# Layer 2's attention and its products: the planner's order replaced by a pipeline laid by hand

## The chip, the cores and the metric

The kernel runs on one core of a Trainium2 chip. The metric is the device time of one execution in microseconds (us), as a median of several runs.

## What is computed

A two-layer encoder takes one step over T = 576 tokens: 512 new frames of one stream (the prompt) and 64 frames of another that has a past (the sample); the width is 2048. Layer 1 has stick-breaking attention beside a state-space branch. Layer 2 is what the change touches:

```python
def odd_layer(x, past_k, past_v, w_in, rel_bias, w_out, ln_g, ln_b):
    proj = jnp.einsum('bld,de->ble', x, w_in)
    q, k, v, g = jnp.split(proj, 4, axis=-1)
    ...
    o = chunk_band_attention(q, k, v, past_k, past_v, rel_bias).reshape(b_, L, CA_WIDTH) * jax.nn.silu(g)
    mix = jnp.einsum('ble,ed->bld', o, w_out)
    y = layer_norm(DEEPNORM_ALPHA * x + mix, ln_g, ln_b)
```

The attention has 32 heads of 64. Each frame sees its own chunk of 64 frames and the eight before; to the logits a bias by distance is added, then softmax, then the sum over the values. Outputs are y and the new caches of both layers.

## The kernel before

All products run on TensorE (PE) in single precision by halves: a weight `w` is split into `wh` (a copy rounded on ACT, L93) and `wl` (the rest, on DVE, L94), the input x into `yh` and `yl` likewise, and a product is the three terms wh·yh, wh·yl, wl·yh. Activations lie with features on partitions and tokens along the row, so a product of 128 features has 16 blocks of 128 inputs x 3 terms x two halves of 288 tokens: 96 matmuls.

Layer 2's attention runs over 16 pairs of heads. Queries and keys of all pairs have been made before and lie in memory; of the values only pairs 2, 5 and 8 (`VAHEAD`). So there are 29 products in this stage: 13 of values (v) and 16 of gates (g). `run_pairs` (L626) calls for each pair `ca_heads` (L1056: loads queries, keys and the sample's cache, makes the product v, copies it to `vf`, half on DVE at L1079 and half on ACT at L1080, stores it, and turns it to `vt` by transposes at L531 and L534), then `ca_gate` (L1150), then `ca_attend` (L1085). The gates of pairs 9, 11, 13 and 15 (`GLATE`) come after all pairs; the product with the attention's output is then done at the end.

`ca_attend` goes through seven parts: both heads' first 128 queries with the sample's new keys; the sample against its cache; both heads' second 128; and the third and fourth 128 of each head alone. For each part PE makes the logits `z` (L498, L499; the sample's at L504 and L1141), `softmax` takes the minimum of bias minus logits on DVE (L1115), the exponential with its sum on ACT (L1119), reciprocal (L1121) and scaling (L1123) on DVE; PE transposes the weights block by block (`tpw` at L594, the sample's at L600 and L606), and `evict` (L572) copies each transposed tile to `wts` or `wss`, in turn on DVE (L575) and ACT (L577). When all parts are done PE multiplies weights with values (`po` L614, `pos` L623), and `place` (L642) multiplies by the gate `gt` into `of` (L649, L656; without a gate a copy, L647 and L654), which is stored to `o_scr`.

The PSUM has eight banks of 512 columns. Four of them (`pj`) are three banks for halves of products (`product_halves`, L1015: first tokens 0 to 287 over all inputs, then the others) and one more for transposing (`spare`, in turn with the bank "t" by `tbank`, L580); the pool `pmc` has two for logits ("s"), one for transposing and the sample's `pos` ("t"), and one for `po` and the values' transposes ("o"). A gate is the silu of its product in six steps over ACT and DVE (`silu_halves`, L1032, the last at L1042).

The order on each engine is not that of the code: a planner takes, among the instructions that are ready by its own estimate of times, in order of the code's priority, so that products slide between the attention's instructions. What is written sets priorities, buffers and dependences. Behind the stage stands `mix_norm` (L750): it loads the stored outputs again (`bring`: `ol` at L773, split on ACT at L774 and DVE at L775), multiplies by `w_out` and normalises. The loads `ol8` to `ol15` go where the input x lay, which is free once the last product of the stage has been made.

Of the kernel before, what the change touches and what calls it, by code (L numbers as in the profile page):

```python
# [7 lines left out]
F32 = mybir.dt.float32  # L8
F32R = mybir.dt.float32r
AF = mybir.ActivationFunctionType  # L10
ALU = mybir.AluOpType
# [3 lines left out]
P = 128  # L15
# [34 lines left out]
def encoder(ctx: ExitStack, tc: tile.TileContext, a):  # L50
# [125 lines left out]
    def seven(wa, m0, wb, m1, sums, ps, tmp, last=False, early=None):  # L176
# [16 lines left out]

        a11, a21, a22 = raw(wa, m0, 0, "sr", tmp, 4), raw(wb, m1, 0, "sr", tmp, 4), raw(wb, m1, 1, "sr", tmp, 4)
        s_ = raw(None, 0, 0, "raw", wpool, 2)
        pa, pc = bank("pa", 2), bank("pc")
        o0, o1 = (tmp.tile([P, T], F32, tag="so", name="so", bufs=4) for _ in range(2))
# [374 lines left out]
    def evict(dst, src):  # L572
        flip[0] ^= 1
        if flip[0] & 1:
            nc.vector.tensor_copy(dst, src)  # L575
        else:
            act(dst, src, AF.Copy)  # L577

    spare = []

    def tbank(name):

        if spare:
            flip[0] ^= 2
            if flip[0] & 2:
                return spare[0]
        return pm.tile([P, 512], F32, tag="t", name=name)

    def transpose_tile(wsrc, r, t, wts, flipq=False):

        nb = t + 1
        tp = tbank("tpw")
# [5 lines left out]
    def transpose_new(wsrc, dst):  # L598
        tp = tbank("tpn")
# [3 lines left out]
    def transpose_cached(wsrc, dst):  # L603
        tp = tbank("tpw")
# [409 lines left out]
    turn_ = [0]  # L1014

    def product_halves(w, m):

        ws = [wparts(w, m, u) for u in range(2)]
        accs = []
        for v in (H0, H1):  # L1020
            acc = hbanks[turn_[0] % 3]
            turn_[0] += 1
            for u, (wh, wl) in enumerate(ws):
                for k in range(8):
                    c = slice(k * P, (k + 1) * P)
                    x, y = xh[8 * u + k][:, v], xl[8 * u + k][:, v]
                    for i, (st, mv) in enumerate(((wh, x), (wh, y), (wl, x))):
                        mm(acc, st[:, c], mv, start=(u == 0 and k == 0 and i == 0), stop=(u == 1 and k == 7 and i == 2))  # L1028
            accs.append((v, acc))
        return accs  # L1030

    def silu_halves(pl, accs, dst, tag):  # L1032
        t = pl.tile([P, 580], F32, tag=tag, name=tag, bufs=2)[:, :T]
        for v, p in accs:
            act(t[:, v], p, AF.Abs)
        act(t, t, AF.Exp, scale=-1.0)
        act(t, t, AF.Ln, bias=one1)
        for v, p in accs:
# [232 lines left out]
```

## Time and profile before

| what | us |
|---|---|
| median of 3 runs | 2790.82 (2788.62 to 2793.09) |
| the profiled execution | 2791.59 |
| its span, first to last instruction | 2789.8 |
| PE busy in the span | 2662.2 |
| layer 1's attention (695 to 1150): length, PE busy | 455.0, 449.16 |
| layer 2's attention with its products (1924.2 to 2547.5): length, PE busy | 623.3, 575.01 |
| from its last attention to `mix_norm`'s products (2487.6 to 2547.5): length, PE busy | 59.9, 48.98 |

Engines are PE (matmul), PEld (PE's loading of weights, beside it), DVE, ACT, POOL and SP. Matmuls are pipelined, so their durations overlap: the distance from one start to the next is what one costs. PEclk is TensorE's granted clock as a share of 2.4 GHz; its lower level is 1.2 GHz. "Idle before <- X" is the time that an engine stood still before an instruction, and X what ended it.

### The profile page before, as it was taken

The page shows a single profiled execution, that of the slowest core. Times are in us where ns is not written, and L with a number is a line of the kernel's source. Part 1 is how long each engine was busy: PE and PEld are TensorE (multiplying, and loading weights), DVE is VectorE, ACT ScalarE, POOL GpSimd, SP SyncE. Part 2 cuts the span into 40 slices and gives each one's busy share as a digit, 9 for nine tenths or more (in the row PEclk, how much of TensorE's full clock was granted, in tenths as well). Part 3 has the DMA queues.
Part 4 walks back from the last instruction along what each step waited for, and adds up shares of the span by engine and source line. Part 5 has one row for each costly group of instructions (what it writes and reads, how often), then busy time and mean ns, then how long its engine had stood idle before and what let it go on. Part 6 is the DMA issues. An engine that isn't in the chain of part 4 may idle for free.

```text
span 2789.8 us, 47678 instructions
## 1 busy us (share of the span) xinstructions
PE 2662.2 (95%) x19742; PEld 2538.9 (91%) x19742; DVE 1610.5 (58%) x2520; ACT 1190.2 (43%) x1993; POOL 63.4 (2%) x140
## 2 busy tenths in 40 slices
PE   8999999999999999999997799999999999989996
PEld 8999898999999999999997799999788888878995
DVE  6666656665666766733358377765554455443447
ACT  5434343443555655621136234444444444433224
POOL 0000000000000000000000000000000000000004
PEclk9999999999999999999998899999999999999998
DMA  5222222323323222533345465455644555434333
GB/s 184 76 90 76 71 94 65 101 70 117 97 90 99 93 90 92 191 106 101 94 129 186 138 210 161 158 162 179 199 152 147 155 159 162 143 107 139 104 102 134
DMA packets 148761, 350.36 MB, mean 126 GB/s; under 512 B 26304, under 2 KB 43968, under 8 KB 148544
## 3 DMA queue, kind: packets, MB, share of 16 engines
q1 hardware_dynamic: 105696, 281.68, 32.9%
q10 hardware_dynamic: 42848, 65.63, 6.3%
q8 instruction: 155, 2.54, 0.4%
q14 instruction: 62, 0.51, 0.1%
HBM read 281.63 MB, written 65.61 MB: 124 GB/s over the span
## 4 chain that ended last, share of the span: by engine, by line
PE 87%; DVE 5%; DMA 3%; ACT 3%; issue 2%; SPq 0%; ACTq 0%; DVEq 0%
PE pj L124 48%; PE pj L1028 13%; PE pa L159 5%; PE pc L159 3%; PE po L614 2%; PE pj L853 2%; PE pb L159 1%; PE tpw L594 1%; PE px L124 1%; ACT wh L93 1%; DVE wl L94 1%; PE z L498 1%; PE pos L623 1%; PE z L499 1%; DMA sr<-w_in 1%
## 5 line engine op out<-in xcount | busy, mean ns | idle before, releaser
L94 DVE TENSOR_TENSOR wl<-raw,wh 128x1024 fp32r<-128x1024 f32 x372 | 456.4, 1227 | 518.0 <-ACT wh L93 516.7
L93 ACT ACTIVATE wh<-raw 128x1024 fp32r<-128x1024 f32 x372 | 393.6, 1058 | 801.5 <-PE pj L124 498.1
L1028 PE MATMUL pj<-yh,wh 128*128 128x288 f32 x928 | 286.4, 309 | 18.9 <-DVE gt L1042 16.3
L1028 PE MATMUL pj<-yh,wl 128*128 128x288 f32 x928 | 283.7, 306 | 0.0
L1028 PE MATMUL pj<-yl,wh 128*128 128x288 f32 x928 | 282.9, 305 | 0.0
L1028 PEld LDWEIGHTS pj<-yh,wh 128*128 128x128 f32 x928 | 182.6, 197 | 27.5 <-DVE gt L1042 18.2
L124 PE MATMUL pj<-oh,wh 128*128 128x288 f32 x960 | 205.8, 296 | 0.0
L124 PE MATMUL pj<-ol,wh 128*128 128x288 f32 x960 | 205.8, 296 | 0.0
L124 PE MATMUL pj<-oh,wl 128*128 128x288 f32 x960 | 205.5, 295 | 0.0
L1028 PEld LDWEIGHTS pj<-yl,wh 128*128 128x128 f32 x928 | 182.3, 196 | 0.8
L1028 PEld LDWEIGHTS pj<-yh,wl 128*128 128x128 f32 x928 | 182.0, 196 | 0.5
L124 PEld LDWEIGHTS pj<-oh,wl 128*128 128x128 f32 x960 | 155.0, 188 | 0.0
L124 PEld LDWEIGHTS pj<-oh,wh 128*128 128x128 f32 x960 | 154.8, 188 | 0.2
L124 PEld LDWEIGHTS pj<-ol,wh 128*128 128x128 f32 x960 | 154.6, 188 | 0.0
L1119 ACT ACTIVATE t<-t,smx 128x128 f32<-128x128 f32 (+3 forms) x128 | 71.2, 557 | 88.4 <-DVE smx L1115 70.8
L1115 DVE CUSTOM_DVE_ANT_0 t<-z,bp 128x128 f32<-128x128 f32 (+3 forms) x128 | 60.2, 486 | 30.4 <-PE tpw L594 11.8
L498 PE MATMUL z<-kh,q 128*128 128x128 f32 (+1 forms) x192 | 66.5, 357 | 11.5 <-DVE smx L1115 9.3
L802 DVE TENSOR_TENSOR d<-xr,pj 128x576 f32<-128x576 f32 (+3 forms) x30 | 20.2, 673 | 91.5 <-PE pj L124 83.8
L93 ACT ACTIVATE wh<-sr 128x1024 fp32r<-128x1024 f32 x43 | 45.1, 1057 | 63.9 <-PE pc L159 23.2
L614 PE MATMUL po<-wts,vt 128*64 128x384 f32 (+3 forms) x384 | 70.8, 441 | 1.1 <-DVE wts L575 1.1
L577 ACT ACTIVATE wts<-tpw 128x128 f32<-128x128 f32 (+1 forms) x96 | 41.3, 430 | 60.9 <-PE tpw L594 53.5
L499 PE MATMUL z<-kl,q 128*128 128x128 f32 (+1 forms) x192 | 61.1, 328 | 0.0
(568 smaller groups left out, 7227.7 us busy)
## 6 DMA issues: line engine op xcount, KB each, us to landing
raw<-w_in SPq DMA_DIRECT2D x234, 512.0 KB, 3.6
raw<-w_out SPq DMA_DIRECT2D x95, 512.0 KB, 3.5
sr<-w_in SPq DMA_DIRECT2D x48, 512.0 KB, 4.3
ol<-o_scr SPq DMA_DIRECT2D x40, 288.0 KB, 5.4
xr<-xT SPq DMA_DIRECT2D x29, 288.0 KB, 5.8
q<-q_scr SPq DMA_DIRECT2D x64, 128.0 KB, 3.1
kh<-k_scr SPq DMA_DIRECT2D x64, 128.0 KB, 3.2
o_scr<-of ACTq DMA_DIRECT2D x24, 288.0 KB, 2.8
```

The lines of the kernel that those rows point to most:

```text
L93: act(hi, src, AF.Copy)
L94: tt(lo, src, hi.bitcast(F32), ALU.subtract)
L124: mm(ps[:, at.start + v.start:at.start + v.stop], st[:, c], mv[u * 8 + k][:, v], start=(first and k == 0 and i == 0), stop=(last and k == ...
L159: mm(acc, st[:, c], mv, start=(first and k == 0 and i == 0), stop=(k == 7 and i == 2), skip_group_check=more)
L498: mm(dst, q, kh, start=True, stop=False)
L499: mm(dst, q, kl, start=False, stop=True)
L577: act(dst, src, AF.Copy)
L614: mm(po[q, b * P:TP], vt[:, b, q], wts[:, b, r, b * P:TP], start=(b == 0), stop=(b == 3))
L853: mm(ps[i], st[:, c], mv, start=(u == order[0] and k == 0 and j == 0), stop=(u == 0 and k == 7 and j == 2))
L1028: mm(acc, st[:, c], mv, start=(u == 0 and k == 0 and i == 0), stop=(u == 1 and k == 7 and i == 2))
L1115: nc.vector.tensor_tensor_reduce(t[:, i, at:at + z.shape[1]], z, b, -1.0, 3e38 if j == 0 else sm[:, i:i + 1], ALU.add, ALU.min, sm[:, i:i ...
L1119: act(t[:, i, :], t[:, i, :], AF.Exp, scale=-1.0, bias=sm[:, i:i + 1], accum_out=sm[:, 2 + i:3 + i])
```

## The change

`ca_heads` only loads. All products come from a generator `ca_fill`, in the order v0 g0 v1 g1 g2 v3 g3 and so on, the four late gates at the end; it is advanced by an eighth of a product (12 matmuls) at a time. A product is made whole, both halves of 288 tokens in one tile of two banks, and two such tiles take the four banks of `pj`: the third half bank and the second transposing bank are gone. `ca_attend` calls `slot` after the logits and softmax of each part: it advances the generator by 13/7 of an eighth on the mean, and does the transposes that the slot before has left; the transposes of this part wait for the next slot. Values times weights and `place` of a pair (`finish`) are done in the first slot of the next pair. Gates have two buffers (`gt`) instead of one, the values' copy is one on DVE, silu goes over whole rows. Each late gate is multiplied in as soon as its product is there.

```diff
-        tp = tbank("tpw")
+        tp = pm.tile([P, 512], F32, tag="t", name="tpw")
...
-    x0, x1 = (pj.tile([P, 1024], F32, tag="pj", name="pj") for _ in range(2))
-    hbanks, second = [x0[:, 0:HALF], x0[:, 512:512 + HALF], x1[:, 0:HALF]], x1[:, 512:1024]
...
+    def ca_fill():
+        todo = []
+        for pr in range(NPAIR_CA):
+            todo += ([] if pr in VAHEAD else [("v", pr)]) + ([] if pr in GLATE else [("g", pr)])
+        for kind, pr in todo + [("g", pr) for pr in GLATE]:
+            ps = pj.tile([P, 1024], F32, tag="pj", name="pj")
+            toks, at = parts(HALF)
+            for u in range(2):
+                wh, wl = wparts(a["w_in1"], (32 if kind == "v" else 48) + pr, u)
+                for k in range(8):
+                    c = slice(k * P, (k + 1) * P)
+                    for i, (st, mv) in enumerate(((wh, xh), (wh, xl), (wl, xh))):
+                        for v in toks:
+                            mm(ps[:, at.start + v.start:at.start + v.stop], st[:, c], mv[u * 8 + k][:, v],
+                               start=(u == 0 and k == 0 and i == 0), stop=(u == 1 and k == 7 and i == 2))
+                    if k % 2 and (u, k) != (1, 7):
+                        yield
+            if kind == "v":
+                vf = ce_.tile([P, T], F32, tag="kvf", name="vf", bufs=2)
+                nc.vector.tensor_copy(vf, ps[:, at])
+                store(a["o_cav"][pr], vf)
+                yield
+                vts[pr] = turned_values(c_, vf)
+            else:
+                gt = cl_.tile([P, T], F32, tag="gt", name="gt", bufs=2)
+                silu(cl_, ps[:, at], gt, T, "st")
+                if pr in GLATE:
+                    tt(outs[pr], outs[pr], gt, ALU.mult)
+                    store(o_scr1[pr], outs[pr])
...
-            for i in range(np_):
-                transpose_tile(tv[:, i, :], seg[i][0], seg[i][1], wts, True)
+            slot([lambda i=i, tv=tv, seg=seg: transpose_tile(tv[:, i, :], seg[i][0], seg[i][1], weights()[0], True)
+                  for i in range(np_)])
...
+    def slot(work):
+        todo, later[:] = list(later), work
+        due[0] += 13
+        n, due[0] = due[0] // 7, due[0] % 7
+        for i in range(max(n, len(todo))):
+            if i < n:
+                next(fill, None)
+            if i < len(todo):
+                todo[i]()
...
+        finish = ca_attend(pr, st, slot)
+        later.append(finish)
+    slot([])
+    for _ in fill:
+        pass
```

On PE, the place in before that the trace shows at 2173.8 us: the transpose of a sample's new weights (L600), two heads' logits (L498, L499), transposes (L594), the next pair's first logits, and then a product again.

```order
L1028 MATMUL pj<-yh,wl 128x288
L600 MATMUL tpn<-cst,tsm 64x128
L498 MATMUL z<-kh_19286,q_21611 128x384
L499 MATMUL z<-kl_19288,q_21611 128x384
L498 MATMUL z<-kh_19287,q_21618 128x384
L499 MATMUL z<-kl_19289,q_21618 128x384
L594 MATMUL tpw<-cst,t 128x128 x6
L498 MATMUL z<-kh_19292,q_22032 128x128
L499 MATMUL z<-kl_19294,q_22032 128x128
...
L1141 MATMUL z<-kf,qb 128x64
L1028 MATMUL pj<-yh,wh 128x288
```

Such places stand between products that go by halves; the number of products' matmuls between two parts is the planner's.

On PE after the change, in the middle of the stage: two parts (L1131 ends the first's logits, L590 and L584 are transposes) with products (L1044) ahead of each transpose.

```order
L596 MATMUL tpw<-cst,tsm 128x128 x4
L498 MATMUL z<-kh_19290,q_22041 128x128
L499 MATMUL z<-kl_19292,q_22041 128x128
L498 MATMUL z<-kh_19291,q_22048 128x128
L499 MATMUL z<-kl_19293,q_22048 128x128
L1131 MATMUL z<-kf,qb 128x64
L1044 MATMUL pj<-yh,wl 128x288
...
L590 MATMUL tpn<-cst,tsm 64x128
L1044 MATMUL pj<-yl,wh 128x288 x2
...
L584 MATMUL tpw<-cst,t 128x128 x2
```

Some twenty matmuls of a product stand now between logits and the transposes that follow. Just ahead of that place, one of six stretches of the changed order in which the attention stands without products, where values times weights (L604, L613) of the pair before come too.

```order
L584 MATMUL tpw<-cst,t 128x128 x6
L604 MATMUL po<-wts,vt 64x512
L498 MATMUL z<-kh_19284,q_21653 128x384
L499 MATMUL z<-kl_19286,q_21653 128x384
L498 MATMUL z<-kh_19285,q_21660 128x384
L499 MATMUL z<-kl_19287,q_21660 128x384
L604 MATMUL po<-wts,vt 64x512
L604 MATMUL po<-wts,vt 64x384 x2
...
L613 MATMUL pos<-wss,cv 64x64 x8
L613 MATMUL pos<-wss,vt 64x64 x2
L531 MATMUL tpv<-cst,vf 128x128 x4
```

The products that stood here have moved ahead, and the stretch is 31 to 65 instructions long at its six places.

On DVE, before, at a gate's last step (L1042, two halves), between a part's softmax steps (L1115, L1123):

```order
L1123 TENSOR_SCALAR t<-t,smx 128x512
L1039 SCALAR_TENSOR_TENSOR st<-pj,st 128x288 x2
L1115 ISA t,smx<-z,bp_19301 128x384
L1115 ISA smx 128x1
L1042 TENSOR_TENSOR gt<-pj,st 128x288 x2
L575 COPY wts<-pj 128x128
```

and after, at the same step of a gate (L135, whole):

```order
L1113 TENSOR_SCALAR t<-t,smx 128x512
L1111 RECIPROCAL smx<-smx 128x1
L639 TENSOR_TENSOR of<-po,gt 128x512
L1113 TENSOR_SCALAR t<-t,smx 128x512
L646 TENSOR_TENSOR of<-pos,gt 128x64
L135 TENSOR_TENSOR gt<-pj,st 128x576
L575 COPY wts<-tpw 128x128
```

The gate's last step, which frees its product's banks, now stands behind `of` of an earlier pair, whose gate's buffer it takes.

On PE at the end of the stage, before: the last transposes and values of the attention, and then the late gates' products (286 matmuls from L1028 on).

```order
L594 MATMUL pj<-cst,t 128x128 x3
L623 MATMUL pos<-wss,cv 64x64 x8
L623 MATMUL pos<-wss,vt 64x64 x2
L614 MATMUL po<-wts,vt 64x512 x2
L614 MATMUL po<-wts,vt 64x384 x2
L614 MATMUL po<-wts,vt 64x256 x2
L614 MATMUL po<-wts,vt 64x128 x2
L1028 MATMUL pj<-yh,wh 128x288
```

and after: the last product's end (L1044), with what follows of pairs 13 to 15, and the first products of `mix_norm` (L124).

```order
L1044 MATMUL pj<-yh,wl 128x288 x2
L584 MATMUL tpw<-cst,t 128x128 x3
L604 MATMUL po<-wts,vt 64x512
L498 MATMUL z<-kh_19284,q_24722 128x384
...
L1131 MATMUL z<-kf,qb 128x64
...
L124 MATMUL pj<-oh_25775,wh 128x288 x4
...
L584 MATMUL tpw<-cst,t 128x128 x18
L604 MATMUL po<-wts,vt 64x512 x2
...
L124 MATMUL px<-oh_25775,wh 128x288 x2
```

The late gates' products have moved ahead of the last two pairs' attention, of which some 95 rows stand behind the last product.

## Rows read from the trace of the kernel before

**Rows 1.** The page: busy time of PE, and its clock in 40 slices.
```profile
PE 2662.2 (95%) x19742; PEld 2538.9 (91%) x19742; DVE 1610.5 (58%) x2520; ACT 1190.2 (43%) x1993; POOL 63.4 (2%) x140
...
PEclk9999999999999999999998899999999999999998
```

**Rows 2.** Windows: length, busy PE, PEld, DVE, ACT, POOL (x instructions), PEclk, DMA, GB/s.
```profile
695.00:1150.00 455.00, 449.16 (x3443) 427.48 (x3441) 301.35 (x469) 271.62 (x477) 0.00 (x0) 1.00 0.29 92
...
1924.20:2547.50 623.30, 575.01 (x4178) 520.88 (x4177) 307.88 (x862) 256.15 (x611) 2.00 (x6) 0.96 0.50 152
...
2487.60:2547.50 59.90, 48.98 (x338) 48.51 (x336) 21.16 (x30) 19.22 (x28) 0.00 (x0) 0.89 0.29 98
```

**Rows 3.** Windows: products alone, and the stage's products (L1028 only).
```profile
1890.00:1910.00 20.00, 20.00 (x153) 20.00 (x152) 14.67 (x19) 10.94 (x19) 0.52 (x1) 1.00 0.37 125
...
1924.20:2547.50 623.30, 414.75 (x2784) 392.46 (x2784) 0.96 0.50 152
```

**Rows 4.** PE's waits, us, times, longest: 1910 to 2550, then 695 to 1150.
```profile
PE pj L1028 <- DVE gt L1042: 16.3, 8, 6.0
PE z L498 <- DVE smx L1115: 9.3, 16, 1.5
PE tpw L594 <- ACT wss L577: 5.2, 7, 1.0
PE tpw L594 <- ACT wts L577: 4.9, 8, 1.5
PE pj L594 <- DVE wts L575: 3.0, 3, 1.5
...
PE pj L124 <- DVE kf L561: 3.4, 3, 1.1
```

**Rows 5.** Timeline of PE from 2173 us: start, duration, instruction, idle before it.
```profile
2173.76 0.27 PE L600 MATMUL tpn<-cst,tsm 128*64 128x128 f32 x1
...
2175.44 0.44 PE L594 MATMUL tpw<-cst,t 128*128 128x128 f32 x2 [0.71 <-ACT wss L577]
...
2179.66 0.40 PE L1028 MATMUL pj<-yh,wh 128*128 128x288 f32 x1 [1.12 <-DVE gt L1042]
2179.90 0.41 PE L1028 MATMUL pj<-yl,wh 128*128 128x288 f32 x1
```

**Rows 6.** Groups of DVE and ACT, 1924.2 to 2488: busy us, mean ns.
```profile
L1115 DVE CUSTOM_DVE_ANT_0 t<-z,bp 128x128 f32<-128x128 f32 (+3 forms) x128 | 60.2, 486 | 30.4 <-PE tpw L594 11.8 <-DMA bp<-relb 7.6 <-PE z L499 5.5
L1123 DVE TENSOR_SCALAR t<-t,smx 128x128 f32<-128x128 f32 (+3 forms) x128 | 46.1, 384 | 2.1
L575 DVE COPY wts<-pj 128x128 f32<-128x128 f32 (+1 forms) x64 | 31.1, 486 | 43.3 <-PE pj L594 43.1
...
L775 DVE TENSOR_TENSOR ol<-ol,oh 128x576 fp32r<-128x576 f32 x1 | 0.8, 757 | 0.0
...
L1119 ACT ACTIVATE t<-t,smx 128x128 f32<-128x128 f32 (+3 forms) x128 | 71.2, 557 | 88.4 <-DVE smx L1115 70.8 <-DMA ckr<-cak 9.8 <-DVE smx L1121 4.0
```

**Rows 7.** A window of 20 us, one of ten with a dip.
```profile
2370.00:2390.00 20.00, 17.47 (x108) 16.44 (x107) 6.58 (x15) 8.18 (x19) 0.00 (x0) 0.83 0.52 155
```

**Rows 8.** Windows: two stretches without products, and the last attention.
```profile
2066.00:2079.20 13.20, 9.92 (x62) 7.13 (x61) 11.46 (x42) 10.16 (x28) 0.00 (x0) 0.81 0.58 169
2173.80:2179.70 5.90, 2.93 (x19) 2.00 (x17) 3.65 (x9) 5.19 (x11) 0.00 (x0) 1.00 0.79 230
...
2478.60:2487.60 9.00, 7.45 (x66) 4.71 (x64) 4.24 (x10) 5.02 (x12) 0.00 (x0) 1.00 0.20 66
```

**Rows 9.** Chain that ends last, 2480 to 2560: start, duration, piece.
```profile
2489.55 4.62 DMA ol<-o_scr
...
2500.23 14.65 PE pj L1028 x95
...
2519.96 27.69 PE pj L1028 x191
```

**Rows 10.** The page's DMA issues: KB each, us to landing.
```profile
ol<-o_scr SPq DMA_DIRECT2D x40, 288.0 KB, 5.4
```

More of the change, by code (lines that the diff above doesn't have):

```diff
@@ L192, in out @@
                 tt(dst, u1, src, ALU.add)
+        o0, o1 = (tmp.tile([P, T], F32, tag="so", name="so", bufs=4) for _ in range(2))
         a11, a21, a22 = raw(wa, m0, 0, "sr", tmp, 4), raw(wb, m1, 0, "sr", tmp, 4), raw(wb, m1, 1, "sr", tmp, 4)
@@ L598, in transpose_new @@
     def transpose_new(wsrc, dst):
-        tp = tbank("tpn")
+        tp = pm.tile([P, 512], F32, tag="t", name="tpn")
         nc.tensor.transpose(tp[0:TS, 0:P], wsrc, ident)
@@ L603, in transpose_cached @@
     def transpose_cached(wsrc, dst):
-        tp = tbank("tpw")
+        tp = pm.tile([P, 512], F32, tag="t", name="tpw")
         for b in range(4):
@@ L1008, in encoder @@
     tp7.release()
-    x0, x1 = (pj.tile([P, 1024], F32, tag="pj", name="pj") for _ in range(2))
-    hbanks, second = [x0[:, 0:HALF], x0[:, 512:512 + HALF], x1[:, 0:HALF]], x1[:, 512:1024]
[L1014 to L1038, printed above, removed]
-            stt(t[:, v], p, 0.0, t[:, v], ALU.min, ALU.subtract)
-        act(t, t, AF.Exp)
-        for v, p in accs:
-            tt(dst[:, v], p, t[:, v], ALU.mult)
     pm = pool("pmc", bufs=1, space=PSUM)
-    spare.append(second)
     ce_ = pool("cae", bufs=1, side="left")
@@ L1103, in ca_attend, with weights @@
         store(a["o_cavo"][pr], cv)
-        wts = c_.tile([P, 4, 2, TP], F32, tag="wts", name="wts")
-        wss = c_.tile([P, 5, P], F32, tag="wss", name="wss")
+        w = {}
+        def weights():
+            if not w:
+                w["p"] = c_.tile([P, 4, 2, TP], F32, tag="wts", name="wts")
+                w["s"] = c_.tile([P, 5, P], F32, tag="wss", name="wss")
+            return w["p"], w["s"]
         tsm = c_.tile([P, T], F32, tag="tsm", name="tsm")
@@ L1144, in ca_attend, with finish @@
             softmax(tv, [[(0, z[:, i * n:i * n + n], bp[seg[i][0]][:, TP - n:TP])] for i in range(np_)], n)
[L1145 to L1156 removed]
+            slot([lambda i=i, tv=tv, seg=seg: transpose_tile(tv[:, i, :], seg[i][0], seg[i][1], weights()[0], True)
+                  for i in range(np_)])
+        def finish():
+            while not (pr in vts and (pr in gts or pr in GLATE)):
+                next(fill)
+            wts, wss = weights()
+            vt, gt = vts.pop(pr), gts.pop(pr, None)
+            outs[pr] = place(cl_, gt, prompt_pv(wts, vt), lambda: sample_pv(
+                [(wss[:, b, :], cv[:, b, :]) for b in range(4)] + [(wss[0:TS, 4, :], vt[0:TS, 4, :])]), True)
+            if gt is not None:
+                store(o_scr1[pr], outs[pr])
+        return finish
+    later, due = [], [0]
+    def slot(work):
[7 more added lines that the diff above has]
+                todo[i]()
+    for pr in range(NPAIR_CA):
+        st = ca_heads(pr)
+        if pr in VAHEAD:
+            vf = ce_.tile([P, T], F32, tag="kvf", name="vf", bufs=2)
+            load(vf, v_scr[VAHEAD.index(pr)])
+            vts[pr] = turned_values(c_, vf)
+        finish = ca_attend(pr, st, slot)
[3 more added lines that the diff above has]
+        pass
     cl_.release()
```

44 lines of the change are left out of this document (11 added, 33 removed).

## The prediction

> **What bounds the kernel now.** I read the page first: PE is busy 95% of the span, and the row of its granted clock is full nearly everywhere but in the second half [rows 1]. So the kernel is bound by TensorE, and only two things can move its time: stretches in which PE has nothing to do, and stretches in which it runs at the lower of its two clocks. Both are read stage by stage in the table of windows. Layer 1's attention (695 to 1150 us) is 455 us long with PE busy 449.16 and the clock at 1.00. The stage that the change touches, layer 2's attention with its products, is 1924.2 to 2547.5 us: 623.3 us, PE busy 575.01, clock 0.96 [rows 2]. That is 48.3 us of idle PE, and 0.04 x 623.3 = 24.9 us given to the clock: **73.2 us lost in this stage**, against 5.8 us idle in the 455 us of layer 1's. What surrounds the stage is the same code in the same order, so it is left as it is.
>
> The products are 2784 matmuls [rows 3]. Where only products run, one takes 20.00 / 153 = 0.131 us [rows 3], so they are 364.7 us of the stage. The rest of its PE time, 623.3 - 73.2 - 364.7 = 185.4 us, is attention: 11.6 us of PE work for each of 16 pairs, 1.66 us for each of the seven parts of a pair.
>
> Where do the 48.3 us lie? The list of PE's waits names the gate first: 16.3 us in 8 waits for `gt` (L1042), then 9.3 us for the softmax's minimum, which frees a logits bank, then three kinds of transposes that wait for an eviction, 5.2 + 4.9 + 3.0 = 13.1 us [rows 4]. The timeline shows how they hang together: at 2173.76 the products stop; for 5.9 us there are only logits and transposes, each waiting for softmax or eviction of the part just before, and the next product starts at 2179.66 when the gate of an earlier product is done [rows 5]. In this stretch PE works 2.93 us of 5.9. A part's own chain is long: minimum 486 ns, exponential 557, scaling 384 and an eviction of 486 [rows 6], with small steps between them; without products in between PE sits it out. After such a stretch the products come at 0.24 us [rows 5] instead of 0.131, the lower clock (1.2 GHz instead of 2.4), so a stretch costs twice. In twenty-microsecond windows I count ten dips, each right behind a stretch without products; the window at 2370 (0.83) is one of them [rows 7]. The ten cost the 24.9 us of clock above, 2.5 us each.
>
> **The change part by part.** *Products between logits and transposes.* The new code puts about 13/7 of a product's eighths behind each part's logits, some 22 matmuls or 2.9 us, and transposes the part before only then. The chain from logits to scaled weights (486 + 557 + 384 ns = 1.4 us, some 2 with the small steps) fits under it. The row that it is nearest to is layer 1's attention, in which products stand beside softmax in the same way and only one transposing bank exists: 5.8 us lost in 455, and PE's longest waits there are for `kf`, 3.4 us [rows 2, 4]. I take **6 us** for all covered slots of the new stage. Bounds: nothing, and 25 us (second rival).
>
> *Stretches that stay uncovered.* The order of the changed kernel shows that the planner doesn't keep this spacing. It pulls products ahead until their banks are held, and in six places of the PE's order 31 to 65 instructions of attention stand with no product among them, some 29 parts in all, the tail not counted. What holds the banks is the gate: there are now two `gt` buffers, the third gate's last step on DVE stands behind the `of` of an earlier pair, and with it that product's PSUM tile. How long a part takes without cover is read from before: 13.2 us for about 6 parts, 5.9 for about 2.5 [rows 8]: 2.2 to 2.4, and I take 2.2 us, from the longer of the two. A part is 1.66 us of PE work, so 29 x (2.2 - 1.66) = **16 us**. Bounds: 1.8 us, PE nearly full because transposes now belong to the part before; and 3 us, most of the chain laid bare (486 + 557 + 384 + 486 ns = 1.9 us, and logits, transposes and the small steps to that).
>
> *The tail.* Before, the four late gates run after the attention: from 2487.6 to 2547.5 PE is busy 48.98 of 59.9 us at clock 0.89 [rows 2], and the chain shows what it waits for: a load `ol` of 4.62 us, then 95 matmuls in 14.65 and 191 in 27.69 with a gate ahead of each [rows 9]. So 10.9 us idle and 6.6 of clock are lost there today. After, the late gates are pulled ahead, the products end before pair 15 has begun, and about 2.1 pairs of attention remain with nothing to cover them. DVE has first the splits of the loads `ol8` to `ol12`, which can't start before the last product has freed its inputs: 5.4 us from issue to landing [rows 10], six steps of 0.757 for the first one's half on ACT (taken at the DVE's price) and five splits on DVE [rows 6], and 0.5 for the first eviction: 10.4 us, with the issue 10.8. Then nine parts of 2.2 = 19.8, the last transposes, values and placing 5, and the first late `ol` load with its split 6: 41.6 us, in which PE works 2.1 x 11.6 = 24.4. Lost: **17 us**. The gain of the four gates' cover is thus spent where today's tail stood.
>
> *Clock.* Six uncovered stretches, one dip each as today: 6 x 2.5 = **15 us**. The trace of layer 1's attention has its transposes among products at clock 1.00, and the stretch at 2478.6, nearly all transposes and values, is itself at 1.00 [rows 2, 8]; the drop is seen behind it. The Trainium skill, "TensorE: Matmul & The Clock Gate", Part 4 (PE-mode transpose), states that transposes do not count as PE being busy for the clock. By that rule the tail with its rows of transposes would bring two dips more, and the sum would be 5 us higher; this trace neither confirms nor refutes it, as its transposes stand either among products or in stretches that also idle.
>
> *What costs nothing.* A product's two halves now share one PSUM tile: same matmuls, same columns, no change on PE. The values' copy is one on DVE instead of half there and half on ACT, silu works on whole rows: a few tenths of a microsecond a product on engines that are busy 308 and 256 us of 623 [rows 2]; if that cover is gone it shows as a longer part, which is in the bounds of 2.2. The second transposing bank goes: in the covered slots its price is in the 6 us.
>
> Sum: 6 + 16 + 17 + 15 = 54 us lost instead of 73.2, a gain of 19. The profiled execution took 2791.6 us (span 2789.8, and 1.8 around it), 0.8 more than the median. So 2791.6 - 19.2 - 0.8 = **2772 us**.
>
> **Rivals.** *First, the uncovered stretches run nearly full*, since a part's transposes now wait for softmax of the part before and not of its own. At 1.8 us a part: 29 x 0.14 = 4, tail 13.6, covered 6, two dips 5, together 28.6: 2746 us. For it speaks that layer 1 hardly loses anything; against it that both stretches measured need 2.2 or more.
>
> *Second, no change: one transposing bank.* Each pair evicts ten transposed tiles, 160 in all, and today's waits of transposes on evictions (13.1 us, [rows 4]) exist with two banks. If each eviction lays bare a quarter of its 0.49 us, 160 x 0.12 = 19 us come on top of the covered 6, all losses are 73, and the time is 2791 us. Against it: layer 1 has the one bank and its trace shows next to no wait for an eviction; but there the parts have more products around them.
>
> *Third, slower: the uncovered parts lay bare the chain.* The transposes wait for DVE, and DVE has `of`, the gate and the splits of weights queued ahead. At 3.0 us a part: 29 x 1.34 = 39, tail 24, covered 6, eight dips 20, together 89: 2807 us. The point from which it decides: 6 + 29 (t - 1.66) + (9 t - 2.6) + 15 = 73.2, so t = 2.7 us. For it speaks the 2.36 of the stretch at 2173.8 and that these stretches are longer than any today; against it that the longer one is at 2.2 with a wait for the gate within.
>
> **How the numbers follow.** The forecast (2763 to 2783: a part from 2.0 to 2.5 us) gets 0.46, the first rival 0.20, the second 0.17, the third 0.17. About 0.2%, 5.6 us, is what a measurement of this kernel can tell from no change. Faster: 0.46 + 0.20 = 0.66; same: 0.17; slower: 0.17. The range runs from the first rival's value, half of which lies below it (2746), to the third at 2.9 us a part (2803).
>
> **What would show it.** In the changed trace the stage from 1924 us to the first products of `mix_norm` should be some 19 us shorter, PE's wait for `gt` gone from the list, and the waits of transposes for evictions or softmax gathered in six stretches without products, with a dip of the clock behind each. In between, the twenty-microsecond windows should stand at 1.00 and nearly full. The tail from the last product on should take about 42 us. I am wrong if transposes wait in the covered slots too (second rival), if a part without products is well under or over 2.2 us, if dips come without such stretches, or if the first pairs of the stage wait for loads that now come before their products.

## The result, and the profile after

The changed kernel takes **2761.33 us** in the median of 4 runs (2757.11 to 2767.02), against 2791.95 us for the kernel before beside it: a ratio of 0.9893, with an interval of 0.9872 to 0.9914, 30.6 us faster. The profiled execution took 2762.77 us with a span of 2760.8, 29.0 shorter than before's.

The table of windows of the changed kernel (length, busy time of PE, PEld, DVE, ACT and POOL with the number of instructions, granted clock, DMA share, GB/s): the stage up to the end of its last product; from there to the steady products of `mix_norm`; and a stretch of 635.8 us from 1924.2, where before's stage begins, which is given for before and after. The first fence is after, the second before.

```profile
1924.20:2470.40 546.20, 529.16 (x3940) 489.23 (x3939) 283.39 (x753) 232.97 (x527) 0.29 (x2) 0.99 0.53 163
2470.40:2523.80 53.40, 37.64 (x216) 24.72 (x214) 29.44 (x79) 22.72 (x57) 0.00 (x0) 0.78 0.35 111
...
1924.20:2560.00 635.80, 602.96 (x4427) 550.06 (x4426) 325.51 (x845) 266.05 (x596) 0.29 (x2) 0.98 0.51 159
```

```profile
1924.20:2560.00 635.80, 586.03 (x4257) 531.43 (x4257) 317.32 (x876) 265.15 (x624) 2.00 (x6) 0.96 0.51 155
```

Layer 1's attention is as it was, PE busy 449.15 of its 455.0 us [rows 2]. Over the 635.8 us PE stands idle for 32.8 us instead of 49.8. The trace's spells at the lower clock add up to 30.7 us there, instead of 51.2, and half of a spell is lost: 15.4 instead of 25.6. Together 48.2 us are lost where 75.4 were, 27.2 less.

The 29.0 us by which the span is shorter do not all lie there. With the two traces matched by the number of the matmul, the stage and its `mix_norm` (from the 14001st matmul, just ahead of the stage's first product, to `mix_norm`'s last) take 794.0 us before and 771.2 after. These 22.8 us are less than 27.2, since PE's busy time, counted at the full clock, is 4.5 us longer there (723.1 instead of 718.6). Another 10.2 us lie ahead of the stage, between the 11001st and the 12001st matmul (175.2 and 165.0), where the products of layer 2's queries and keys begin. Ahead of these two pieces the changed execution is 4.7 us longer, with more spells at the lower clock; behind them it is 0.7 shorter.

The 10.2 us belong to an edit that the description of the change does not name: in `seven`, which makes the queries and keys, two tiles are allocated ahead of the first weights (`sr`) instead of behind them.

```diff
+        o0, o1 = (tmp.tile([P, T], F32, tag="so", name="so", bufs=4) for _ in range(2))
         a11, a21, a22 = raw(wa, m0, 0, "sr", tmp, 4), raw(wb, m1, 0, "sr", tmp, 4), raw(wb, m1, 1, "sr", tmp, 4)
...
-        o0, o1 = (tmp.tile([P, T], F32, tag="so", name="so", bufs=4) for _ in range(2))
```

Before, the loads of these weights (L182) wait 26.5 us for the stores of `stage`, a tile of the products ahead (the longer kind is shown). After, a load into `so` (L209) waits in their place, the weights' loads wait for these stores only 1.3 us in all, and PE's longest wait there falls from 12.9 to 2.7 us. The waits are those of SPq, the queue of loads, between 1500 and 1590 us, and of PE between 1540 and 1610 (us in all, times, longest; in each fence before, then after):

```profile
SPq L182 <- DMA o_cav<-stage: 14.5, 2, 13.9
SPq L209 <- DMA v_scr<-stage: 23.4, 1, 23.4
```

```profile
PE pc L159 <- ACT wh L93: 12.9, 1, 12.9
PE pc L159 <- ACT wh L93: 2.7, 1, 2.7
```

No run moved these lines by themselves. But the piece takes 164.4 to 165.5 us in the traces of the changed kernel and the six runs below that are made from it, and 173.9 to 175.5 in those of the kernel before and the six made from that. Times of the stage with `mix_norm` are therefore given beside the medians in what follows. They are of one execution each, and executions of one kernel lie up to 10 us apart.

PE's waits between 1910 and 2550 us (what waits, for what, us in all, times, longest), beside [rows 4]:

```profile
PE tpw L584 <- DVE wts L575: 8.8, 13, 2.0
PE z L498 <- DVE smx L1105: 5.8, 7, 2.6
PE tpw L584 <- ACT wts L577: 5.6, 5, 1.5
...
PE pj L1044 <- DVE gt L135: 0.9, 3, 0.3
```

The wait of a product for a gate has gone from 16.3 us to 0.9. Transposes still wait for evictions (14.4 us in the two lines shown, 13.1 in the three of before), and logits for a minimum (5.8 instead of 9.3). In the stage ahead of its tail nearly all of PE's idle time lies in six stretches without products. Four of them by windows:

```profile
2179.00:2189.60 10.60, 8.88 (x65) 5.59 (x63) 9.09 (x26) 7.93 (x18) 0.00 (x0) 1.00 0.62 189
2204.20:2218.40 14.20, 10.80 (x74) 6.86 (x71) 11.66 (x41) 8.11 (x23) 0.00 (x0) 1.00 0.50 154
2283.90:2297.10 13.20, 10.37 (x77) 6.92 (x76) 10.53 (x35) 6.22 (x17) 0.00 (x0) 1.00 0.64 197
2347.40:2366.10 18.70, 13.79 (x85) 9.29 (x85) 12.82 (x44) 8.37 (x25) 0.00 (x0) 0.91 0.49 154
```

The other two, from 2105.3 and 2432.9, are 8.3 and 7.7 us long with PE busy 7.17 and 6.88 and the clock at 1.00. All six are 72.7 us long with PE busy 57.9, so 14.8 of the 17.0 us that PE idles in the stage before its tail lie in them. Only the longest has the clock below 1.

### The profile page after: what moved, and what is told of

The parts are those of the page before. It is cut to its first block, busy times and chain, and to the rows that moved or that the text cites. A ratio compares the mean times of both kernels' runs of the same rounds, so it can differ in the third digit from the quotient of the medians.

```text
span 2760.8 us, 47573 instructions
## 1 busy us (share of the span) xinstructions
PE 2660.5 (96%) x19742; PEld 2538.6 (92%) x19742; DVE 1616.7 (59%) x2488; ACT 1187.8 (43%) x1964; POOL 63.4 (2%) x140
## 3 DMA queue, kind: packets, MB, share of 16 engines
q1 hardware_dynamic: 105696, 281.68, 32.8%
## 4 chain that ended last, share of the span: by engine, by line
PE 87%; DVE 5%; DMA 3%; issue 2%; ACT 2%; SPq 0%; ACTq 0%; DVEq 0%
PE pj L124 49%; PE pj L1044 12%; PE pa L159 5%; PE pc L159 3%; PE po L604 3%; PE tpw L584 2%; PE pj L843 2%; PE pb L159 2%; PE px L124 1%; DVE wl L94 1%; PE z L498 1%; PE z L499 1%; DMA raw<-w_in 1%; ACT wh L93 1%; PE pos L613 1%
## 5 line engine op out<-in xcount | busy, mean ns | idle before, releaser
L124 PE MATMUL pj<-oh,wh 128*128 128x288 f32 x960 | 205.5, 296 | 2.8 <-ACT oh L764 2.8
L1044 PE MATMUL pj<-yh,wh 128*128 128x288 f32 x928 | 206.5, 300 | 1.4 <-DVE gt L135 0.9
L124 PE MATMUL pj<-ol,wh 128*128 128x288 f32 x960 | 205.6, 296 | 0.0
L1044 PE MATMUL pj<-yh,wl 128*128 128x288 f32 x928 | 205.5, 298 | 0.0
L124 PE MATMUL pj<-oh,wl 128*128 128x288 f32 x960 | 205.4, 295 | 0.0
L1044 PE MATMUL pj<-yl,wh 128*128 128x288 f32 x928 | 203.7, 299 | 0.0
L124 PEld LDWEIGHTS pj<-oh,wh 128*128 128x128 f32 x960 | 154.7, 188 | 3.3 <-ACT oh L764 3.0
L1044 PEld LDWEIGHTS pj<-yh,wh 128*128 128x128 f32 x928 | 151.5, 189 | 3.7 <-DVE gt L135 1.6
L124 PEld LDWEIGHTS pj<-oh,wl 128*128 128x128 f32 x960 | 154.9, 188 | 0.0
L124 PEld LDWEIGHTS pj<-ol,wh 128*128 128x128 f32 x960 | 154.5, 188 | 0.1
L1044 PEld LDWEIGHTS pj<-yl,wh 128*128 128x128 f32 x928 | 150.9, 189 | 1.9 <-issue 0.8
L1044 PEld LDWEIGHTS pj<-yh,wl 128*128 128x128 f32 x928 | 151.7, 189 | 1.0
L575 DVE COPY wts<-tpw 128x128 f32<-128x128 f32 (+1 forms) x96 | 46.9, 488 | 95.6 <-PE tpw L584 95.2
L604 PE MATMUL po<-wts,vt 128*64 128x512 f32 (+3 forms) x384 | 84.1, 454 | 1.0 <-ACT wts L577 1.0
L584 PE MATMUL tpw<-cst,t 128*128 128x128 f32 x320 | 60.8, 291 | 16.0 <-DVE wts L575 8.8
L498 PE MATMUL z<-kh,q 128*128 128x128 f32 (+1 forms) x192 | 65.8, 356 | 6.5 <-DVE smx L1105 5.8
```

The costliest lines, as they stand in the source:

```text
L124: mm(ps[:, at.start + v.start:at.start + v.stop], st[:, c], mv[u * 8 + k][:, v], start=(first and k == 0 and i == 0), stop=(last and k == ...
L498: mm(dst, q, kh, start=True, stop=False)
L584: nc.tensor.transpose(tp[:, b * P:(b + 1) * P], wsrc[:, b * P:(b + 1) * P], ident)
L604: mm(po[q, b * P:TP], vt[:, b, q], wts[:, b, r, b * P:TP], start=(b == 0), stop=(b == 3))
L1044: mm(ps[:, at.start + v.start:at.start + v.stop], st[:, c], mv[u * 8 + k][:, v], start=(u == 0 and k == 0 and i == 0), stop=(u == 1 and k ...
```

## The experiments

The question was which part of the change brings the 30 us. Beside the moved allocation it has three: the slots that lay products by hand beside the attention, the delay of the transposes, and the banks (a second whole product instead of three half banks and a second transposing bank). Each run is compared with the kernel before on its chip, whose medians lay between 2791.95 and 2795.32 us.

**The banks alone.** In the kernel before, products are made whole (`product`), the second transposing bank goes, gates get two buffers; no generator and no slots.

```diff
...
-        accs = product_halves(a["w_in1"], 48 + pr)
-        gt = lt.tile([P, T], F32, tag="gt", name="gt", bufs=1)
-        silu_halves(lt, accs, gt, "st")
+        pg = product(a["w_in1"], 48 + pr, 2, xh, xl)
+        gt = lt.tile([P, T], F32, tag="gt", name="gt", bufs=2)
+        silu(lt, pg, gt, T, "st")
```

> The kernel before with one part of the change alone: products whole, two of them in flight in the four banks of pj, one transposing bank, two gate buffers, silu and the values' copy over whole rows. The order stays the planner's, with no slots, no generator, and gates and values made per pair. Theory (half the gain is the next product no longer waiting for a gate to read its half bank, 16.3 us of idle PE before; the rest is the slots, which keep products beside the attention): about 2775 us, the list of waits without gt, but more dips of the clock than after. Rival 1 (the slots do it all): 2785 to 2795, the idle time moved from gt to evictions. Rival 2 (the banks do it all): 2757 to 2765.

Measured: 2763.97 us, ratio 0.9898 (0.9882 to 0.9915). That is the changed kernel's time within the scatter, and without the moved allocation: the banks alone bring at least what the three parts bring together, the second rival. In the traces the stage with `mix_norm` takes 771.1 us here and 771.2 in the changed kernel. By the medians the banks alone (29.1 us) and the moved allocation (10.2 in the traces) would make more than the 30.6 of the whole change. Whether slots and delay cost the difference or scatter makes it is open.

**The slots' products undone.** The two lines in `slot` that advance the generator are taken out of the changed kernel.

```diff
-            if i < n:
-                next(fill, None)
```

> The changed kernel with one part undone: slots still delay the transposes, but no longer advance the products; a pair's products are made in the code only when finish needs them, and the planner alone slides them between the attention. Theory (the slots' products are what keeps the attention covered): slower than the changed kernel by some 10 us, 2768 to 2778, and equal to the planner's order with whole products within 5 us. Rival (the delay of the transposes to the next slot is what counts): as the changed kernel, 2757 to 2767.

Measured: 2757.62 us, 0.987 (0.9854 to 0.9886), no slower than the changed kernel. The planner puts the products beside the attention by itself: with the moved allocation and the delay still in, the stage with `mix_norm` takes 768.6 us. The delay of the transposes was not undone by itself. That it brings anything is not to be seen, since the run of the banks alone has neither slots nor delay.

**What it is in the banks.** Two runs part the fourth half bank from the order of the matmuls. The first:

```diff
-    hbanks, second = [x0[:, 0:HALF], x0[:, 512:512 + HALF], x1[:, 0:HALF]], x1[:, 512:1024]
+    hbanks = [x[:, o:o + HALF] for x in (x0, x1) for o in (0, 512)]
...
-            acc = hbanks[turn_[0] % 3]
+            acc = hbanks[turn_[0] % 4]
...
-    spare.append(second)
```

> The kernel before with one thing changed: the bank that served as second transposing bank is a fourth half bank for products. Products stay by halves, gates have one buffer, the order is the planner's. Theory (what the change gains, it gains because a whole product can be made while the gate before it is still read from its banks): PE's wait for gt falls from 16.3 us to under 4, and the time is 2765 to 2776 us. Rival (it is the order of the matmuls, both halves of the tokens for each weight in turn, which frees the weights of the first half of the inputs half a product earlier): the wait for gt stays or turns into one for evictions, 2786 to 2795.

Measured: 2761.52 us, 0.9881 (0.9867 to 0.9895). The second:

```diff
-        for v in (H0, H1):
-            acc = hbanks[turn_[0] % 3]
-            ...
+        for u in range(2):
+            wh, wl = wparts(w, m, u)
+            for k in range(8):
+                ...
+                    for v, acc in accs:
```

> The kernel before with the other thing alone: three half banks and the second transposing bank stay, but a product goes through its weights once, with both halves of the tokens for each, so the first half of the weights is free half a product earlier. Theory (banks): no gain, 2786 to 2797 us, since a product needs two free half banks at its start and one of three is still read by the gate; the wait for gt stays above 10 us. Rival (order of the matmuls): 2760 to 2772.

Measured: 2797.26 us, 1.001 (0.9999 to 1.0021): nothing. PE's wait for `gt` in the two runs, the fourth bank first:

```profile
PE pj L1028 <- DVE gt L1042: 1.4, 5, 0.3
```

```profile
PE pj L1028 <- DVE gt L1042: 15.8, 6, 6.6
```

Three changed lines do what the whole change does, and more in the stage (765.8 us with `mix_norm`), and the wait for `gt` goes with them. With it go spells at the lower clock. In before six of the stage's ten spells begin within a wait for `gt` or at most 1 us behind it; they are 27.3 us long and so cost 13.7. Together with the 16.3 us of the waits themselves that is 30 us, close to the 33.8 that this run gives back.

**The gate's buffers.** The prediction held that a gate tile keeps a product's banks. The run of the banks alone with one buffer instead of two, and the changed kernel with three:

```diff
-        gt = lt.tile([P, T], F32, tag="gt", name="gt", bufs=2)
+        gt = lt.tile([P, T], F32, tag="gt", name="gt", bufs=1)
```

> The kernel before with whole products and one transposing bank (as in the run of the banks alone), but one gate buffer instead of two: the gate buffers by themselves. Theory (a gate's last step waits for the pair whose gate's buffer it takes, and holds its product's banks): 4 to 12 us slower than with two buffers, 2768 to 2776 us, with more stretches in which PE waits for gt. Rival (the gate's buffer decides nothing): 2760 to 2768, the same within 4 us.

```diff
...
-                gt = cl_.tile([P, T], F32, tag="gt", name="gt", bufs=2)
-                silu(cl_, ps[:, at], gt, T, "st")
+                gt = cl_.tile([P, T], F32, tag="gt", name="gt", bufs=3)
+                silu(cl_, ps[:, at], gt, T, "st", 1)
```

> The changed kernel with three gate buffers, paid for with one buffer instead of two for silu's work tile. In PE's order the six stretches without products in the middle become four, but 87 instead of 68 instructions stand behind the last product. Theory of the prediction (the gate tile holds the product's banks and so makes the stretches): idle PE before the tail falls from 17 to about 12 us and the time by 3 to 8 us, 2753 to 2758. Rival (products that are let go earlier run out earlier, and the tail takes it back): 2759 to 2768.

Measured: 2758.71 (0.9874, 0.9858 to 0.989) and 2759.18 us (0.9875, 0.9857 to 0.9892). With one, two and three buffers the time stays between 2758 and 2764, so the gate's buffers decide nothing that can be measured; the third was paid for with a work tile of silu, so that run is not of the buffers alone. The traces show that a gate's buffer does hold its banks where the prediction said so. The gate's last step starts within 0.15 us of the end of an earlier pair's `of` for 13 of 16 gates with one buffer, for 7 in the changed kernel with two and for 1 with three, but for none in before (the nearest starts 1.5 us behind). The time does not follow, as PE's waits for `gt` are 3.0 us at most in these kernels.

**The hold itself.** In before 4.3 to 21.4 us pass from silu's first step on a half of a gate to its last, 7.1 in the median. If a fourth bank helps because a gate's banks are held through silu, then shortening the hold must help as well.

```diff
-        silu_halves(lt, accs, gt, "st")
+        raw = lt.tile([P, 580], F32, tag="gr", name="gr", bufs=1)[:, :T]
+        for v, p in accs:
+            nc.vector.tensor_copy(raw[:, v], p)
+        silu_halves(lt, [(v, raw[:, v]) for v, _ in accs], gt, "st")
```

> The kernel before, with three half banks and the second transposing bank as they are, but each half of a gate's product is copied out of its bank by DVE as soon as it is made, and silu works on the copy: the bank is held for one copy of some 0.45 us instead of through silu's six steps. Theory (it is the time for which a gate's banks are held that stops the products; the fourth half bank helps because it lets PE go on through that time): PE's wait for gt is gone, the time 2762 to 2776 us. Rival (only a bank more lets whole products overlap, however short the gate's reading; or a second transposing bank costs more than it gives): 2785 to 2797.

Measured: **2716.15 us** (2715.33 to 2716.56), 0.9722 (0.9708 to 0.9737): 77.6 us faster than before and 45 faster than the changed kernel. The two longest of PE's four kinds of waits between 1910 and 2550 us (the others are 0.7 and 0.5 us, and none is for `gt`), the window of 635.8 us, and the copy's group among DVE's:

```profile
PE z L498 <- DVE smx L1115: 2.4, 4, 1.5
PE pj L1028 <- DVE gr L1155: 1.1, 1, 1.1
...
```

```profile
1924.20:2560.00 635.80, 630.79 (x4813) 592.01 (x4812) 361.07 (x944) 285.28 (x641) 2.01 (x6) 0.99 0.54 168
```

```profile
L1155 DVE COPY gr<-pj 128x288 f32<-128x288 f32 x32 | 14.2, 456 | 30.2 <-PE pj L1028 30.1
```

PE idles 5.0 us instead of 49.8, and one spell of 6.8 us at the lower clock is left of 51.2. The copies cost DVE 14.2 us that it had. The stage with `mix_norm` takes 719.6 us instead of 794.0: 67.0 us less are lost, and PE's busy time, counted at the full clock, is 7.5 us shorter. But this is more than the wait for `gt` and its spells, and more than either expectation; a shorter hold and a bank more ought to be two ways to the same end. The last run puts both together:

> The kernel before with both single edits together: the second transposing bank becomes a fourth half bank for products, and each half of a gate's product is copied out of its bank at once. With before, the fourth bank alone and the copy alone this makes a table of two by two. Theory A (only the time for which a gate holds its banks counts, so with the copy a bank more neither helps nor harms): 2712 to 2721 us. Theory B (with more room products run further ahead of the attention, until they wait for buffers of values and gates, and stretches of attention stay behind without cover; three half banks and the copy keep them spread): slower than the copy alone, 2735 to 2760 us, with waits for evictions in such stretches and dips of the clock in the tail.

Measured: 2768.06 us, 0.9912 (0.9897 to 0.9927), slower than the copy alone as in Theory B, and over its range. The fourth bank takes back 52 of the copy's 78 us:

| us | a second transposing bank | a fourth half bank |
|---|---|---|
| gate read in its bank | 2791.95 to 2795.32 | 2761.52 |
| gate copied out | 2716.15 | 2768.06 |

So room for products helped here where a gate holds its bank, and harmed where it is copied out. In the last cell the copy is not always made at once, however. It has one buffer, `gr`, which the gate before reads until its last step (L1042), and with a fourth bank that step starts right behind an earlier pair's `of` (L656) for 11 of 16 gates. On DVE:

```profile
2158.59 0.23 DVE L656 TENSOR_TENSOR of<-pos,gt 128x64 f32<-128x64 f32 x1
2158.85 0.83 DVE L1042 TENSOR_TENSOR gt<-gr,st 128x288 f32<-128x288 f32 x2
2159.72 0.82 DVE L1154 COPY gr<-pj 128x288 f32<-128x288 f32 x2
```

For six of 16 gates the copies end 7 to 30 us behind the product, with the copy alone none more than 4.3. This is not what costs the time, as PE's waits for `gr` are 1.3 us in all. The traces give another reason. I counted the products' matmuls that are done when the first logits on the sample's new keys of a pair start, divided by 96.

| pair (of 16) | 4th | 8th | 12th | 16th |
|---|---|---|---|---|
| before | 5.0 | 12.0 | 18.0 | 24.0 |
| copy alone | 5.5 | 13.0 | 19.0 | 25.0 |
| fourth bank alone | 7.2 | 14.2 | 21.0 | 27.0 |
| fourth bank and copy | 7.1 | 15.2 | 21.2 | 28.0 |
| the change | 7.1 | 15.4 | 22.5 | 29.0 |

There are 29 products. With four half banks or two whole ones some 1.7 more of them are made at the fourth pair than with the copy alone and two to four more at the last, where two, one or none are left. With three half banks and the copy they keep the attention's pace, and four products, some 50 us, are left for the end. The kernel with both has its waits where the changed kernel has them, in stretches of attention without products; the window of 635.8 us, and the longest of its waits:

```profile
1924.20:2560.00 635.80, 603.45 (x4406) 550.99 (x4405) 335.89 (x915) 272.94 (x628) 2.00 (x6) 0.97 0.51 160
```

```profile
PE tpw L594 <- DVE wts L575: 7.2, 13, 1.2
```

That the run ahead makes the stretches is read from this table and the order; no run changed it alone with all else equal. The next one tried to.

**Products held back by hand.** In the changed kernel a one-column addition ahead of each weight's split waits for the softmax of a part, so that a product can't begin long before its share.

```diff
+                raw = fetch(a["w_in1"], (32 if kind == "v" else 48) + pr, u)
+                hold(raw, nth, u)
+                wh, wl = split(wpool, raw, [P, 1024], "w")
...
+        at = (2 * p + u) * 112 // 58 - 6
+        if at >= 0:
+            stt(raw[:, 0:1], marks[min(at, len(marks) - 1)], 0.0, raw[:, 0:1], ALU.mult, ALU.add)
```

> The changed kernel with each half of a product held back: a one-column addition on DVE makes the split of its weights wait for the softmax of a part that lies six parts before its even share (112 parts over 58 halves), so that the planner cannot pull products ahead. In PE's order the six stretches without products become three of 26, 47 and 24 instructions, and the late gates stand among the last two pairs. Theory (the stretches and the tail without cover are what is left to gain; 17 us idle in the stage and 27.5 us idle or at the lower clock in the tail): 10 to 20 us faster than the changed kernel, 2741 to 2752. Rival (the held splits come late and PE waits for wh or wl instead, or the loads of mix_norm that wait for the last product take the tail's place): no gain, 2758 to 2770, with PE waiting for ACT wh L93 and DMA ol.

Measured: 2763.09 us, 0.9896 (0.9879 to 0.9913): no gain. At the last pair 27.7 products were made instead of 29.0, so it held them back only by 1.3. Idle time and clock cost 44.0 us in the window of 635.8 us instead of 48.2, but the stage with `mix_norm` takes 774.2 us. The waits that the rival named are not there either (0.7 us for `wh`, none for `ol`). It fails to settle the point.

**Attention with nothing beside it.** To see what a part takes without cover:

```diff
-                        for v in toks:
+                        for v in toks if (u, k, i) in ((0, 0, 0), (1, 7, 2)) else ():
```

> The changed kernel without the matmuls of layer 2's products but for the first and last four of each (116 of 2784 are left), so the attention, its loads, the splits of the weights and the gates run with nothing to cover them: this measures the time of a part without cover, over 112 parts. Theory: 2.2 us a part as in the two stretches of the kernel before, so 246 us and 15 for what is left of the products and the first loads, 255 to 275 us from the first logits to mix_norm, with a clock well under 1. First rival: 1.8 us a part, about 217 us. Third rival: 3 us, the whole chain, about 350 us.

Measured, in one run: the profiled span is 2579.8 us, and from the first logits (1928.4 us) to the last values (2337.7) it is 409 us, 3.7 us a part. The window over 400 us of it:

```profile
1940.00:2340.00 400.00, 295.75 (x1502) 195.28 (x1502) 289.44 (x816) 237.53 (x567) 0.00 (x0) 0.76 0.71 224
```

This is over the third rival's 3 us, but not a pure price of a chain: the clock is at 0.76, the DMA engines are busy 71% of the time instead of 51, and 20 us are waits of what is left of the products for split weights. I take it as an upper bound of a part without cover; no run shows one at the full clock.

**The tail.** In layer 2's `mix_norm` the inputs 1 to 8 change places with 9 to 15, so that those of early pairs go where the stage's input lay, which the last product frees before the attention ends. In the order, products of `mix_norm` then stand between the last pair's transposes. Once on the changed kernel without the slots' products, once on the changed kernel:

```diff
-        bring(ob, range(1, 8))
+        bring(ob, range(1, 8) if inner else range(9, nk))
...
-        bring(orr, range(8, nk))
+        bring(orr, range(8, nk) if inner else range(1, 9))
```

> The changed kernel without products in the slots (as in the run of that name), and in mix_norm of layer 2 the places of the loaded inputs are exchanged: inputs 1 to 8 go where the stage's input lay, which is free when the last product has been made, and 9 to 15 where the attention's tiles lie. In PE's order products of mix_norm (L124) then stand between the last pair's transposes. Theory (what is left to gain lies in the tail without cover): 8 to 16 us faster than without the exchange, 2742 to 2750 us, and the half clock in the tail mostly gone. Rival (the loads and splits of the inputs keep PE waiting and hold up DVE in the tail, so the cover only moves the wait): 2754 to 2762.

> The changed kernel itself with the same exchange of places in mix_norm and nothing else. Theory: 8 to 14 us faster than the changed kernel, 2747 to 2753 us. Rival: 2757 to 2765, the wait of mix_norm's products for their inputs in place of the idle tail.

Measured: 2753.57 us (0.9851, 0.9831 to 0.9871), 4 us better than without, but the intervals overlap, and in the traces the stage with `mix_norm` takes 767.0 us and 768.6, so a gain is not shown; and 2748.15 us (0.9837, 0.9822 to 0.9853), 13 us better than the changed kernel, with the intervals apart. The window of this second run from 2460 to 2520 us, and below it the changed kernel's:

```profile
2460.00:2520.00 60.00, 50.93 (x344) 39.63 (x341) 34.88 (x95) 26.57 (x63) 0.00 (x0) 0.91 0.38 121
```

```profile
2460.00:2520.00 60.00, 46.97 (x287) 34.00 (x285) 36.48 (x104) 26.89 (x68) 0.00 (x0) 0.80 0.32 102
```

In the changed kernel the tail without cover is a real cost: idle 9.1 instead of 13.0 us here, and the clock at 0.91 instead of 0.80. Without the slots' products the same window has the clock at 0.86, and at 0.89 with the exchange.

## Why the prediction was right, and where it was not

Forecast were 2772 us and a gain of 19; measured are 2761 and 31. The direction, and that the gate's wait would vanish, were right, and so was the size in the stage. To `mix_norm`'s steady products it is 18.2 us shorter (605.1 us from 1918.7, where its first product starts, instead of 623.3 [rows 2]), and to `mix_norm`'s last 22.8. What the sum put at nothing is the rest: "What surrounds the stage is the same code in the same order" is wrong by the 10.2 us of the moved allocation. In the stage the sum had 54 us of losses left, and the trace shows 48.2. Before's losses come to 75.4 there instead of 73.2, as the window is 12.5 us longer (1.5 us idle) and the spells cost 25.6 us by themselves instead of 24.9. Against that stand the 4.5 us of longer busy time, for which the sum had no term.

- *The uncovered stretches*: 16 us forecast, 14.8 idle in the six windows. The number and the size were right. The price behind it was right by luck: 72.7 us for 29 parts are 2.5 us a part instead of 2.2, but values times weights stand in them too and keep PE busy for 2.0 us a part instead of 1.66.
- *The covered slots*: 6 forecast, 17.0 - 14.8 = 2.2 us measured. One transposing bank suffices there, and the second rival is out.
- *The clock*: 15 us forecast for a dip behind each of six stretches, and 15.4 measured, but elsewhere. In the stage there are two spells of 3.4 us, one behind the first logits and one in the stretch of 18.7 us; the other five stretches leave the clock at 1.00. The spells of 10.2 and 13.7 us in the tail make up the rest. What failed is the step "one dip each as today". Six of before's ten spells begin within or right behind a wait for the gate, and this wait is gone. The new stretches are also fuller than the one at 2173.8, PE busy 8.88 of 10.6 us instead of 2.93 of 5.9 [rows 8].
- *The tail*: 17 us forecast, 15.8 idle measured; 53.4 us long instead of 41.6, the difference being 0.22 x 53.4 = 11.7 us of clock, which this term did not have. The Trainium skill, "TensorE: Matmul & The Clock Gate", Part 4 (PE-mode transpose), by which transposes don't count as PE being busy, would put dips into the tail, as there are; but a stretch of 10.6 us from 2179.0, with 15 transposes among its 65 matmuls, stays at 1.00, while the tail has 58 among 216. Since the tail is idle as well, no run parts the two.
- *The cause* was wrong. The prediction gave the gain to the slots, "products between logits and transposes", and counted the banks among *what costs nothing*. The runs turn it round: the slots and the delay bring nothing that can be measured, and a fourth half bank alone brings 28.2 us in the stage with `mix_norm`, where the whole change brings 22.8. I had read the 16.3 us of waiting for `gt` as a consequence of stretches without products. The runs show it as a cause: a bank held by the gate stops the products, and freed in either of two ways, by a fourth bank or by an early copy, it gives back 34 or 78 us. Why the copy gives so much more is argued from the table of products made, not shown.
- *What holds the banks* was half right. In the changed kernel seven of 16 last steps start right behind the `of` that frees an earlier gate's buffer, but the number of buffers (one, two and three) does not change the time. In before none does, and what holds the banks there is silu's six steps reading in them.
- *The rivals*: the first forecast 2746 by fuller stretches; they weren't much fuller. That the third stayed away is in the stretches' 2.5 us a part, under the 2.7 at which it would have decided. It isn't in the attention with nothing beside it, where 3.7 were measured.

## What to carry over

Before laying an order by hand, look at what ends the wait for a bank: a PSUM bank that a chain of small steps reads is a bank taken out of the pipeline for the whole chain, and one copy of 0.46 us to SBUF gave here more than a second accumulator and a hand-laid order together. More room is not better by itself: here the planner filled it, and little work was left to cover the end. A change made of several parts is worth taking apart: three lines of this one gain as much in the stage as all of it. And it is worth matching two traces from the first instruction on, since a third of the gain lay in a moved allocation outside the stage.

## What the runs showed of the hardware that was not expected

The clock does not fall behind every stretch in which PE waits: at PE busy 10.37 of 13.2 us, and even 10.80 of 14.2, it stayed at 1.00, while in before it fell within a stretch of 9.92 of 13.2 and behind one of 2.93 of 5.9 (at 2173.8). In the attention with nothing beside it, PE busy 295.75 of 400 us, it stood at 0.76 on the mean. Both 10.80 of 14.2 and 9.92 of 13.2 are three quarters; why the clock fell in the one and not in the other is open.
